# An order of instructions written out by hand and a scheduler, against a recorded one placed by a table of times

## The chip, the cores and the metric

The kernel runs on one core of a Trainium2 chip. The metric is device time in microseconds (us) of one execution; the median of three runs of the kernel before is 1881.01 us (1879.83 to 1881.45). Engines are named TensorE (PE in the profile), VectorE (DVE), ScalarE (ACT), GpSimd (POOL) and SyncE (SP, which only issues DMAs here). Each runs its own queue of instructions in order; semaphores make one wait for another.

## What is computed

A two-layer decoder trunk on x of 2048 positions by 1024 features, in float32. Layer 0 is a gated short convolution; then keys and values are projected once; layer 1 is stick-breaking attention of 8 heads of 64, with a gate.

```python
def _short_conv_mixer(h, w_in, w_conv, w_out):
    b_gate, c_gate, xin, g = jnp.split(h @ w_in, 4, axis=-1)
    y = b_gate * _causal_depthwise_conv(c_gate * xin, w_conv)
    return (y * jax.nn.silu(g)) @ w_out
...
    z = jnp.einsum("bhqd,bhkd->bhqk", qb, kf[:, :, :kl]) * scale
    log_one_minus = jnp.where(mask, jax.nn.log_sigmoid(-z), 0.0)
    rev = lax.cumsum(log_one_minus, axis=3, reverse=True)
    weights = jnp.exp(jnp.where(mask, z + rev, -jnp.inf))
    outs.append(jnp.einsum("bhqk,bhkd->bhqd", weights, vf[:, :, :kl]))
...
    x = x + (o * jax.nn.silu(g)) @ w_out_b[j]
return _rmsnorm(x, norm_f)
```

## The kernel before

Activations lie transposed (features on partitions, positions reversed along the free axis), so the causal sums run forward. Positions are cut into four chunks of 512 (CH). A matmul in full precision is made of three in fp32r: operands are split into a high and a low part (split, L163), and mm3 (L192) adds high x high, high x low, low x high: 24 matmuls of 128 x 512 for 1024 features. Weights are split once and stored to DRAM; later uses load 1 MB of both parts into one of four buffers (whl).

The stages, by function:
- mixer_in (L273) makes the gates C, X, B, G and the convolution: chunks 0 and 1 together (m01), then 2, then 3. Beside m01 run stats_x (square sums of chunks 2 and 3) and fold_gains (weights of later layers scaled and split).
- proj_out (L374) multiplies by w_out_a, adds x, normalizes; proj_k, proj_q, proj_v and proj_gate project, and their results go to DRAM.
- attention(c, h) (L477) takes a chunk of queries and a head, and walks the key chunks kc from c down to 0. For each of four blocks of 128 queries (qi): two matmuls make z (L498, L499); ScalarE makes R and w from it by two sigmoids (L501, L503); GpSimd copies the carry or masks the diagonal (L507 to L511); VectorE runs a multiplying scan over R (L512) and multiplies w by it (L516). Then, for each of four blocks of 128 keys (kb): TensorE transposes the four w into one PSUM bank wt (L524), ScalarE casts it to wth and VectorE makes the rest wtl (L165), and two matmuls add v times each to av (L533, L534).
- out_b and out_norm (L583, L605) are the output projection, the sum of squares, and the last normalization of chunks 0 to 2, where GpSimd multiplies (L612). out_b_last (L623) is chunk 3's: it holds three quarters of the projection, and the last quarter waits for the last head: its output times its gate (L566), 24 matmuls (pol), square sums, normalization, stores.

Rings of buffers limit how far anything runs ahead: z and wt have two PSUM banks each, "lin" two, av one; R 5, w 8, wth and wtl 2, whl 4, "ld" 5, "og" 8, "hl" 1.

What sets the order: every function is a generator that yields an estimate of its matmul time, and merge (L700) draws from several generators in proportion to fixed totals (L732 to L755), so that attention of one chunk stands among projections of the next. Manual dependencies ("pace", L201) hold the filling matmuls near the attention's in the last part. Under this program order a list scheduler with a timing model of its own then reorders the instructions of each engine.

Of the kernel before, what the change touches and what calls it, by code (L numbers as in the profile page):

```python
# [1 line left out]

# [22 lines left out]
F0, F1, F2, F3, F4 = 0.4, 0.5, 0.65, 0.4, 0.6  # L25
S2, S3, S4, S7 = 2.0, 0.5, 3.0, 2.0
YN = 2.0
YP = (10.0, 8.0, 6.0, 6.0)
DLY = 3.0
NB = 3  # L30
GRP, GRY, SLACK = 3, 6, 8
PACE = mybir.DependencyInfo(mybir.DependencyClass.NoSync, mybir.DependencyReason.DATA)

# [3 lines left out]
EPS = 1e-6  # L37

# [7 lines left out]
def kernel(  # L46
# [15 lines left out]
    nc = tc.nc  # L62

    const = ctx.enter_context(tc.tile_pool(name="const", bufs=1))
    psum = ctx.enter_context(tc.tile_pool(name="psum", bufs=2, space=bass.MemoryType.PSUM))
    dram = ctx.enter_context(tc.tile_pool(name="dram", bufs=1, space=bass.MemoryType.DRAM))
    sb = ctx.enter_context(tc.tile_pool(name="sb", bufs=2))

    ident = const.tile([P, P], F32, name="ident")
    make_identity(nc, ident)  # L70
# [116 lines left out]
    MM = 222.0  # L187

    anchors = []
    fine = [24, False]  # L190

    def mm3(ps, wts, a, kt=KD):  # L192

        hi, lo = wts[:, 0], wts[:, 1]
        n = 0
        for k in range(kt):
            for w, m in ((hi, 0), (hi, 1), (lo, 0)):
                ins = nc.tensor.matmul(ps, w[:, k, :], a[k][:, m, :], start=n == 0, stop=n == 3 * kt - 1)  # L198
# [4 lines left out]
                if n % fine[0] == 0 and n < 3 * kt:  # L203
                    yield MM * fine[0]

    def rest(n):
        return MM * (n - (n - 1) // fine[0] * fine[0])

# [40 lines left out]
    def stats_x(c):  # L249
# [6 lines left out]
        yield 1.0  # L256
# [16 lines left out]
    def mixer_in(cs):  # L273
        if len(cs) == 1:
            h[cs[0]] = norm_x(cs[0])
            yield YN * 24 * MM
        for cb in range(KD):
            wts = {}
            for c in cs:
# [5 lines left out]
                def gate(g, i):  # L285
# [16 lines left out]
                    yield from mm3(ps, wts[g], h[c])  # L302
                    return ps

                pc = yield from gate("C", 1)
                cps = t512(f"cs_{nm}")
                nc.scalar.copy(cps, pc)
                yield rest(24)
# [3 lines left out]
                px = yield from gate("X", 2)  # L312
# [3 lines left out]
                if c in late_acc:  # L316
                    if c not in late:
                        pB = yield from gate("B", 0)
                        late[c] = late_rms(c, late_acc[c])
# [3 lines left out]
                yield rest(24)  # L323
                if pB is None:
                    pB = yield from gate("B", 0)
# [7 lines left out]
                yield rest(24)  # L333
                pG = yield from gate("G", 3)
# [10 lines left out]
                yield rest(24)  # L345


    def fold_gains():

        for nm, src, gain in (("kv", w_kv, gains["kv"]), ("b", w_in_b[0], gains["b"])):  # L350
            for i in range(KD):
# [9 lines left out]
                yield 1.0  # L361
        for ob in range(KD):
# [7 lines left out]
            yield 0.5  # L370
# [3 lines left out]
    def proj_out(c):  # L374
# [9 lines left out]
        yield 0.0  # L384
        for ob in range(KD):
            wts = load_w(w_out_a[0][:, ob * P:(ob + 1) * P], ("o", ob), f"o{c}_{ob}")
            ps = lin(f"po_{c}_{ob}")
            yield from mm3(ps, wts, y)
# [6 lines left out]
            yield rest(24)  # L395
# [9 lines left out]
        yield YP[c] * 24 * MM  # L405

    def proj_k(c, kb):
        wts = load_w(None, ("kv", kb), f"k{c}_{kb}")
        ps = lin(f"pk_{c}_{kb}")
        yield from mm3(ps, wts, kept[c])  # L410
# [5 lines left out]
        yield rest(24)  # L416

    def proj_q(c, qb):
        wts = load_w(None, ("b", qb), f"q{c}_{qb}")
        ps = lin(f"pq_{c}_{qb}")  # L420
        yield from mm3(ps, wts, kept[c])
# [3 lines left out]
        yield rest(24)  # L425

    def proj_v(c, vb):
        wts = load_w(None, ("kv", 4 + vb), f"v{c}_{vb}")
        ps = lin(f"pv_{c}_{vb}")
        yield from mm3(ps, wts, kept[c])  # L430
# [7 lines left out]
        nc.sync.dma_start(out=v_d[c][:, :, 2 * vb:2 * vb + 2, :, :], in_=vt.bitcast(F32))  # L438
        yield rest(24) + 2 * MM

    def proj_g(c, gb):
        wts = load_w(None, ("b", 4 + gb), f"gg{c}_{gb}")
        ps = lin(f"pg_{c}_{gb}")
        yield from mm3(ps, wts, kept[c])
# [4 lines left out]
        yield rest(24)  # L449

    def proj_first(c):
        yield from proj_out(c)
        yield from proj_k(c, 0)
        yield from proj_q(c, 0)
        yield from proj_v(c, 0)

    def proj_rest(c):
        yield from proj_k(c, 1)
        yield from proj_q(c, 1)
        yield from proj_v(c, 1)  # L460
        yield from proj_v(c, 2)
        yield from proj_v(c, 3)
        for i in (2, 3):
            yield from proj_k(c, i)
            yield from proj_q(c, i)

    def proj_gate(c, again=True):
# [5 lines left out]
        for i in range(4):  # L473
            yield from proj_g(c, i)


    def attention(c, h, ot):  # L477
# [8 lines left out]
        for kc in range(c, -1, -1):  # L486
# [5 lines left out]
            nc.scalar.dma_start(out=vt.bitcast(F32), in_=v_d[kc][:, :, h, :, :])  # L492
            ws = []
            for qi in range(4):
# [23 lines left out]
                yield (1400.0 if diag else 1800.0) / 4  # L518
            for kb in range(3, -1, -1):
# [14 lines left out]
                ins = nc.tensor.matmul(av[:, 0:n], vs, wl[:, 0:n], start=False, stop=final)  # L534
                anchors.append(ins)
                if kb:
                    yield (1900.0 if diag else 3500.0) / 4
# [5 lines left out]
            yield (1900.0 if diag else 3500.0) / 4  # L543

    def attention_chunk(c, gated=True):
        for hb in range(NH // 2):
            ot = sb.tile([P, CH], F32, name=f"ot_{c}_{hb}", tag="ot", bufs=2)
            yield from attention(c, 2 * hb, ot)
            yield from attention(c, 2 * hb + 1, ot)
            nc.sync.dma_start(out=og_d[c][hb], in_=ot)  # L550
# [22 lines left out]
    def gated_in(c, ks=range(4)):  # L573
# [209 lines left out]
```

## Time and profile before

| | before |
|---|---|
| median of three runs | 1881.01 us |
| the profiled execution, its own time | 1879.53 us |
| its span, first to last instruction | 1877.6 us |
| mean granted TensorE clock | 0.978 |
| instructions | 24847 |
| moved by DMA | 464.63 MB, mean 247 GB/s |

In the table of engines, the busy time of TensorE includes the pipelined end of each matmul; what it can issue is read from start-to-start times. A row of groups has: line, engine, operation, output <- inputs, shape, count, then total busy us and mean ns of one, then the idle time before them and what ended most of it. A row of waits has: engine and line, what it waited for, total us, times, longest. In the timeline each row has start, duration, engine, line, operation, and in brackets the idle time before it and what ended that.

### The profile page before, as it was taken

The numbers are of one execution on the slowest core, as the hardware profiler recorded it, in microseconds if no ns is written. First come the engines' busy times: TensorE is split into PE (matmuls) and PEld (weight loads), VectorE is DVE, ScalarE is ACT, GpSimd is POOL, SyncE is SP. The second block draws the span as 40 slices with busy tenths as digits, with TensorE's granted clock in tenths as the row PEclk, the third lists the DMA queues.
The fourth block names the chain that finished last, engine by engine and source line by source line (L and its number), as shares of the span: only waits on it lengthen the run. The fifth ranks groups of instructions, "written<-read, shape, count | busy, mean of one in ns | idle before, by whom it ended". The sixth has DMA issues, their size and how long they took to land.

```text
span 1877.6 us, 24847 instructions
## 1 busy us (share of the span) xinstructions
PE 1778.2 (95%) x8312; PEld 1448.5 (77%) x8312; DVE 1242.5 (66%) x1830; ACT 773.3 (41%) x1493; POOL 432.9 (23%) x814
## 2 busy tenths in 40 slices
PE   7999999999999999999999999999998998987884
PEld 5888888888778878887888888888776886865573
DVE  7766643554243364478784477787868888799874
ACT  6423311231132142345443344454535555566542
POOL 5000000101021032032221122232223212357533
PEclk9999999999999999999999999999999999998887
DMA  9999995687978697867687765666586666878663
GB/s 295 326 297 326 330 308 168 213 311 277 337 253 285 219 324 264 286 220 250 208 253 237 257 201 187 196 200 214 186 291 202 212 205 233 275 235 261 224 203 131
DMA packets 240783, 464.63 MB, mean 247 GB/s; under 512 B 18704, under 2 KB 133392, under 8 KB 216080
## 3 DMA queue, kind: packets, MB, share of 16 engines
q1 hardware_dynamic: 180576, 404.28, 63.5%
q10 hardware_dynamic: 59920, 58.74, 11.0%
q8 instruction: 66, 1.08, 0.2%
q14 instruction: 61, 0.50, 0.1%
q0 software_dynamic: 160, 0.02, 0.1%
HBM read 326.92 MB, written 136.05 MB: 247 GB/s over the span
## 4 chain that ended last, share of the span: by engine, by line
PE 76%; DMA 9%; DVE 7%; issue 3%; ACT 2%; POOL 2%; SPq 0%; ACTq 0%; POOLq 0%; DVEq 0%
PE pG L198 9%; PE pB L198 9%; PE pX L198 9%; PE po L198 9%; PE pC L198 8%; PE pv L198 5%; PE wt L524 4%; PE pk L198 4%; PE pq L198 4%; PE pg L198 3%; PE av L534 3%; PE av L533 2%; DVE R L512 2%; PE z L498 2%; PE z L499 2%
## 5 line engine op out<-in xcount | busy, mean ns | idle before, releaser
L512 DVE TENSOR_TENSOR_SCAN R<-R,R,ones 128x512 f32<-128x512 f32 x192 | 252.5, 1317 | 32.2 <-ACT R L501 31.7
L501 ACT ACTIVATE R<-z 128x512 f32<-128x512 f32 (+1 forms) x320 | 174.2, 544 | 193.8 <-PE z L499 84.9
L165 DVE TENSOR_TENSOR wtl<-wt,wth 128x512 fp32r<-128x512 f32 (+1 forms) x320 | 186.5, 602 | 81.9 <-ACT wth L164 79.8
L164 ACT CAST wth<-wt 128x512 fp32r<-128x512 f32 (+1 forms) x320 | 160.8, 528 | 185.5 <-PE wt L524 167.4
L516 DVE TENSOR_TENSOR w<-w,R 128x512 f32<-128x512 f32 (+1 forms) x320 | 200.8, 637 | 24.9 <-POOL R L511 4.8
L198 PE MATMUL pC<-h,whl_C 128*128 128x512 f32 x768 | 191.4, 399 | 9.2 <-ACT whl_C L164 7.9
L511 POOL COPY R<-R 128x1 f32<-128x1 f32 x192 | 114.9, 599 | 346.5 <-DVE R L512 313.7
L198 PE MATMUL po<-y,whl_o 128*128 128x512 f32 x768 | 190.7, 394 | 2.7 <-DVE x L392 1.6
L198 PE MATMUL pX<-h,whl_X 128*128 128x512 f32 x768 | 188.1, 393 | 1.1 <-DVE cv L343 1.1
L198 PE MATMUL pG<-h,whl_G 128*128 128x512 f32 x768 | 185.7, 391 | 0.0
L198 PE MATMUL pB<-h,whl_B 128*128 128x512 f32 x768 | 185.6, 391 | 0.0
L524 PE MATMUL wt<-ident,w 128*128 128x128 f32 x1088 | 175.5, 276 | 7.2 <-DVE w L516 5.5
L198 PEld LDWEIGHTS pC<-h,whl_C 128*128 128x128 f32 x768 | 144.6, 191 | 43.6 <-ACT whl_C L164 7.9
L503 ACT ACTIVATE w<-z 128x512 f32<-128x512 f32 (+1 forms) x320 | 172.0, 542 | 2.8 <-PE wt L524 2.7
L198 PEld LDWEIGHTS pX<-h,whl_X 128*128 128x128 f32 x768 | 143.1, 188 | 32.3 <-DVE cv L343 1.3
L198 PEld LDWEIGHTS po<-y,whl_o 128*128 128x128 f32 x768 | 142.4, 188 | 33.2 <-DVE x L392 1.8
L198 PEld LDWEIGHTS pG<-h,whl_G 128*128 128x128 f32 x768 | 143.4, 188 | 30.2 <-issue 0.7
L198 PEld LDWEIGHTS pB<-h,whl_B 128*128 128x128 f32 x768 | 143.4, 188 | 29.8
L524 PEld LDWEIGHTS wt<-ident,w 128*128 128x128 f32 x1088 | 136.8, 142 | 35.7 <-DVE w L516 6.9
L512 DVE TENSOR_TENSOR_SCAN R<-R,ones 128x512 f32<-128x512 f32 (+3 forms) x128 | 117.2, 920 | 45.5 <-POOL R L507 39.2
L534 PE MATMUL av<-wtl,vv 128*128 128x512 f32 (+1 forms) x320 | 125.5, 395 | 19.9 <-DVE wtl L165 19.4
L498 PE MATMUL z<-kt,q 128*128 128x512 f32 (+1 forms) x320 | 128.1, 403 | 7.1 <-ACT w L503 7.0
(161 smaller groups left out, 2662.4 us busy)
## 6 DMA issues: line engine op xcount, KB each, us to landing
whl_o<-sw_o SPq DMA_DIRECT2D x24, 1024.0 KB, 5.3
kt<-k_d ACTq DMA_DIRECT2D x80, 256.0 KB, 3.7
vv<-v_d ACTq DMA_DIRECT2D x80, 256.0 KB, 4.5
whl_C<-sw_C SPq DMA_DIRECT2D x16, 1024.0 KB, 5.3
whl_X<-sw_X SPq DMA_DIRECT2D x16, 1024.0 KB, 5.0
whl_B<-sw_B SPq DMA_DIRECT2D x16, 1024.0 KB, 5.5
whl_G<-sw_G SPq DMA_DIRECT2D x16, 1024.0 KB, 5.4
whl_k<-sw_kv SPq DMA_DIRECT2D x16, 1024.0 KB, 6.7
```

Of the source, the lines that this page charges most:

```text
L164: nc.scalar.copy(hi, src)
L165: eng.tensor_sub(lo, src, hi.bitcast(F32))
L198: ins = nc.tensor.matmul(ps, w[:, k, :], a[k][:, m, :], start=n == 0, stop=n == 3 * kt - 1)
L498: nc.tensor.matmul(ps[:, lom:CH], q2[:, 0, qi * P:(qi + 1) * P], kt[:, lom:CH], start=True, stop=False)
L499: nc.tensor.matmul(ps[:, lom:CH], q2[:, 1, qi * P:(qi + 1) * P], kt[:, lom:CH], start=False, stop=True)
L501: nc.scalar.activation(R[:, lo + 1:CH + 1], ps[:, lo:CH], AF.Sigmoid, scale=-0.125)
L503: nc.scalar.activation(w[:, lo:CH], ps[:, lo:CH], AF.Sigmoid, scale=0.125)
L511: nc.gpsimd.tensor_copy(R[:, 0:1], carry[qi])
L512: nc.vector.tensor_tensor_scan(out=R[:, lo + 1:CH + 1], data0=R[:, lo + 1:CH + 1], data1=ones[:, 0:1].to_broadcast([P, CH - lo]), initial= ...
L516: nc.vector.tensor_mul(w[:, lo:CH], w[:, lo:CH], R[:, lo:CH])
L524: nc.tensor.transpose(wt[:, qi * P:(qi + 1) * P], ws[qi][:, kb * P:(kb + 1) * P], ident)
L534: ins = nc.tensor.matmul(av[:, 0:n], vs, wl[:, 0:n], start=False, stop=final)
```

## The change

The whole body is run once through stand-ins for pools, tiles and engines. They record each operation, with its part (78 names: m01, s2, a35 for chunk 3's head 5, o2 for chunk 2's output, and so on), its dependencies by overlapping regions, and an estimate of its cost. Generators, merge and the manual dependencies are gone. PLAN gives each part two times; a part's operations are spread evenly between them, which gives each a place. Then order() fills a table: again and again it takes, over all engines, the operation that can start earliest (ties by place), given its inputs, its engine, free buffers of its tag, turns between VectorE and GpSimd for operations on two SBUF tiles, and at most 8 DMAs in flight. The result is emitted in that order, under manual_schedule, which keeps it. All instructions therefore carry one line of the program.

```diff
+PLAN = {
+    "m01": (-696.3, -373.1), "s2": (116.9, 307.1), "s3": (-527.4, -474.4), "fold": (141.2, 142.2),
...
+        o.turns = not psum and sum(isinstance(v, View) for v in rest) > 1 and (kind == DVE or kind == POOL and n > 8)
...
+            o.key = t0 + (t1 - t0) * k / count[o.part]
...
+            for e, waiting in avail.items():
+                for o in waiting:
+                    t = max(o.ready, busy[e])
+                    if o.turns:
+                        t = max(t, turn[POOL if e == DVE else DVE])
+                    if o.late is None and len(landing) >= FLY:
+                        t = max(t, landing[-FLY])
+                    for b in o.bases:
+                        if b.tag:
+                            t = max(t, free[b.tag][turn_of[b]]) if turn_of[b] < len(free[b.tag]) else None
+                            if t is None:
+                                break
+                    if t is not None and (best is None or (t, o.place) < best[:2]):
+                        best = t, o.place, o
...
-    v_d = [dram.tile([P, 4, NH, 2, 64], F32, name=f"v_d_{c}") for c in range(NCH)]
+    v_d = [[dram.tile([P, 4, 2, 2, 64], F32, name=f"v_d_{c}_{h}") for h in range(NH // 2)] for c in range(NCH)]
...
+    x2_d = [[dram.tile([P, CH], F32, name=f"x2_d_{c}_{k}") for k in range(KD)] for c in range(NCH)]
...
-                ins = nc.tensor.matmul(ps, w[:, k, :], a[k][:, m, :], start=n == 0, stop=n == 3 * kt - 1)
-                if fine[1] and len(anchors) > SLACK and n % GRP == 0:
-
-                    tc.add_manual_dep(ins.ins, anchors[-1 - SLACK].ins.name, PACE, reason="pace")
+                nc.tensor.matmul(ps, w[:, k, :], a[k][:, m, :], start=n == 0, stop=n == 3 * kt - 1)
...
-            x = ld512(f"x1o_{c}_{ob}")
+            x = sb.tile([P, CH], F32, name=f"x1o_{c}_{ob}", tag="og", bufs=KD)
...
-        sg = load_sg(c, 3)
-        yield -1.0
+        sg = sb.tile([P, CH], F32, name=f"sgl_{c}", tag="hl", bufs=1)
+        nc.sync.dma_start(out=sg, in_=sg_d[c][3])
...
+    part("m01", mixer_in, (0, 1))
...
+    ops = nc.order(PLAN)
+    with tc.manual_schedule():
+        nc.emit(ops)
```

Three places show how rows move. The first is TensorE in chunk 3's head 2, where the key chunk 2 is transposed (wt_3_2_2_3: chunk 3, head 2, key chunk 2, key block 3) and multiplied (av), among the gate projections pg. Before:

```order
L533 MATMUL av_3_2_13846<-wth_3_2_2_3_14033,vv_3_2_2_13974 128x512
L198 MATMUL pg_0_0_14264<-xa_0_0_14246,whl_gg0_0_14262 128x512
L198 MATMUL pg_0_0_14264<-xa_0_1_14247,whl_gg0_0_14262 128x512 x3
L198 MATMUL pg_0_0_14264<-xa_0_2_14248,whl_gg0_0_14262 128x512 x3
L534 MATMUL av_3_2_13846<-wtl_3_2_2_3_14034,vv_3_2_2_13974 128x512
L524 MATMUL wt_3_2_2_1_14069<-ident_66,w_3_2_2_0_13981 128x128
L524 MATMUL wt_3_2_2_1_14069<-ident_66,w_3_2_2_1_13997 128x128
L524 MATMUL wt_3_2_2_1_14069<-ident_66,w_3_2_2_2_14007 128x128
L524 MATMUL wt_3_2_2_1_14069<-ident_66,w_3_2_2_3_14023 128x128
L498 MATMUL z_3_2_0_1_14271<-kt_3_2_0_14232,q2_3_2_13843 128x512
L533 MATMUL av_3_2_13846<-wth_3_2_2_2_14054,vv_3_2_2_13974 128x512
```

The same blocks now:

```order
L350 MATMUL wt_3_2_2_3_14082<-ident_66,w_3_2_2_3_14030 128x128
L350 MATMUL wt_3_2_2_2_14085<-ident_66,w_3_2_2_3_14030 128x128
L350 MATMUL z_3_2_1_2_14113<-kt_3_2_1_13897,q2_3_2_13346 128x512
L350 MATMUL pg_0_0_14110<-xa_0_0_12355,whl_gg0_0_13703 128x512 x2
L350 MATMUL pg_0_0_14110<-xa_0_1_12360,whl_gg0_0_13703 128x512
L350 MATMUL av_3_2_14033<-wth_3_2_2_3_14122,vv_3_2_2_14002 128x512
L350 MATMUL pg_0_0_14110<-xa_0_1_12360,whl_gg0_0_13703 128x512 x2
L350 MATMUL pg_0_0_14110<-xa_0_2_12369,whl_gg0_0_13703 128x512
L350 MATMUL z_3_2_1_3_14142<-kt_3_2_1_13897,q2_3_2_13346 128x512 x2
L350 MATMUL av_3_2_14033<-wtl_3_2_2_3_14135,vv_3_2_2_14002 128x512
L350 MATMUL av_3_2_14033<-wth_3_2_2_2_14126,vv_3_2_2_14002 128x512
L350 MATMUL av_3_2_14033<-wtl_3_2_2_2_14144,vv_3_2_2_14002 128x512
```

Before, the four transposes of one block stood together, and the products of a block came after the next block's transposes. Now both banks are filled at once, w by w, and the products follow after four to eight other matmuls.

The second place is the end of GpSimd's queue: products of chunk 2's output with its norm (x2r_2 by pbs_2), square sums of chunk 3 (acc_x23) and its last products (x2_3 by pbs_3). Before:

```order
L612 TENSOR_TENSOR x2r_2_6_17251<-x2r_2_6_17251,pbs_2_17225 128x512
L612 TENSOR_TENSOR x2r_2_7_17255<-x2r_2_7_17255,pbs_2_17225 128x512
L653 TENSOR_TENSOR acc_x23_0_17435<-acc_x23_0_17435,sq_x232_17454 128x512
L653 TENSOR_TENSOR acc_x23_0_17435<-acc_x23_0_17435,sq_x234_17470 128x512
L664 TENSOR_TENSOR x2_3_1_17118<-x2_3_1_17118,pbs_3_17522 128x512
L664 TENSOR_TENSOR x2_3_4_17121<-x2_3_4_17121,pbs_3_17522 128x512
L664 TENSOR_TENSOR x2_3_7_17124<-x2_3_7_17124,pbs_3_17522 128x512
```

Now:

```order
L350 TENSOR_TENSOR acc_x23_0_17446<-acc_x23_0_17446,sq_x234_17494 128x512
L350 TENSOR_TENSOR x2r_2_0_17412<-x2r_2_0_17412,pbs_2_17522 128x512
L350 TENSOR_TENSOR x2r_2_1_17418<-x2r_2_1_17418,pbs_2_17522 128x512
L350 TENSOR_TENSOR x2r_2_2_17451<-x2r_2_2_17451,pbs_2_17522 128x512
L350 TENSOR_TENSOR x2r_2_3_17482<-x2r_2_3_17482,pbs_2_17522 128x512
L350 TENSOR_TENSOR x2r_2_4_17498<-x2r_2_4_17498,pbs_2_17522 128x512
L350 TENSOR_TENSOR x2r_2_5_17545<-x2r_2_5_17545,pbs_2_17522 128x512
L350 TENSOR_TENSOR x2r_2_6_17550<-x2r_2_6_17550,pbs_2_17522 128x512
L350 TENSOR_TENSOR x2_3_1_16597<-x2_3_1_16597,pbs_3_17566 128x512
L350 TENSOR_TENSOR x2r_2_7_17559<-x2r_2_7_17559,pbs_2_17522 128x512
L350 TENSOR_TENSOR x2_3_4_17005<-x2_3_4_17005,pbs_3_17566 128x512
L350 TENSOR_TENSOR x2_3_7_17404<-x2_3_7_17404,pbs_3_17566 128x512
```

Chunk 2's eight products stood ahead of chunk 3's square sums; now they stand behind them, among the last products.

The third place is the SP queue, where the gate of the last two heads is loaded (sga_3_3 before, sgl_3 now). Before, near the end of its 864 rows, among the stores of chunk 2's output:

```order
L613 DMA out_0_dram<-x2r_2_4_17243 128x512
L611 DMA x2r_2_7_17255<-y_d_2_7_108 128x512
L613 DMA out_0_dram<-x2r_2_5_17247 128x512
L556 DMA sga_3_3_17429<-sg_d_3_3_232 128x512
L613 DMA out_0_dram<-x2r_2_6_17251 128x512
```

Now, 120 rows earlier, ahead of chunk 1's output projection:

```order
L350 DMA x2_d_0_4_249<-x1o_0_4_12656 128x512
L350 DMA sga_3_0_16001<-sg_d_3_0_241 128x512
L350 DMA sgl_3_16054<-sg_d_3_3_244 128x512
L350 DMA ogr_3_0_16061<-og_d_3_0_289 128x512
L350 DMA x1o_0_6_16074<-x1_d_0_6_123 128x512
```

The load no longer stands behind stores that wait for GpSimd.

In the order of heads, chunk 3's head 6 now comes last, after head 7, and chunk 2's output projection stands among chunk 1's and 3's.

More of the change, by code (lines that the diff above doesn't have):

```diff
@@ L1 @@
 from contextlib import ExitStack
+import numpy as np
 import concourse.bass as bass
@@ L37, with __init__, place @@
 EPS = 1e-6
+PLAN = {
[18 rows of a table added]
+}
+PE, ACT, DVE, POOL, SP = "tensor", "scalar", "vector", "gpsimd", "sync"
+SEM = 0.09
+DMA_RATE, DMA_BEFORE, DMA_AFTER, FLY = 0.36, 1.0, 1.4, 8
+class Base:
+    def __init__(self, pool, shape, dtype, kw):
+        self.pool, self.shape, self.dtype, self.kw = pool, list(shape), dtype, kw
+        self.tile = None
+        self.tag = (pool.kind, kw["tag"], kw["bufs"]) if kw.get("bufs") and pool.kind != "dram" else None
+        self.users = []
+    def place(self):
+        if self.tile is None:
+            self.tile = self.pool.real.tile(self.shape, self.dtype, **self.kw)
+        return self.tile
@@ L429, in proj_v @@
         ps = lin(f"pv_{c}_{vb}")
-        yield from mm3(ps, wts, kept[c])
+        mm3(ps, wts, kept[c])
         t = t512(f"vT_{c}_{vb}")
@@ L443, in proj_g @@
         ps = lin(f"pg_{c}_{gb}")
-        yield from mm3(ps, wts, kept[c])
+        mm3(ps, wts, kept[c])
         t = t512(f"sgb_{c}_{gb}")
@@ L448, in proj_g, with proj @@
         nc.sync.dma_start(out=sg_d[c][gb], in_=t)
[L449 to L465, printed above, removed]
+    def proj(c, i):
+        proj_k(c, i)
+        proj_q(c, i)
+        proj_v(c, i)
     def proj_gate(c, again=True):
@@ L533, in attention @@
                 nc.tensor.matmul(av[:, 0:n], vs, wh[:, 0:n], start=first, stop=False)
[L534 to L537, printed above, removed]
+                nc.tensor.matmul(av[:, 0:n], vs, wl[:, 0:n], start=False, stop=final)
             if kc == 0:
```

431 lines of the change are left out of this document (281 added, 150 removed), and 17 rows, old and new, of the table PLAN.

## The prediction

> **What bounds the kernel now.** First the page: the span, the busy shares and the granted clock in 40 slices.
>
> ```profile
> span 1877.6 us, 24847 instructions
> PE 1778.2 (95%) x8312; PEld 1448.5 (77%) x8312; DVE 1242.5 (66%) x1830; ACT 773.3 (41%) x1493; POOL 432.9 (23%) x814
> PEclk9999999999999999999999999999999999998887
> ```
>
> TensorE is busy for 95% of the span; 99.4 us of it is idle, and the clock sags at the end. So the question is where those 99.4 us lie. I cut the span at four matmuls at which each order has done the same TensorE work, with every matmul priced by its start-to-start time. The chain of waits prices a 512-wide matmul, the timeline a transpose:
>
> ```profile
> 57.91 5.44 PE pG L198 x24
> ...
> 1127.59 1.04 PE L524 MATMUL wt<-ident,w 128*128 128x128 f32 x8
> 1128.39 0.48 PE L498 MATMUL z<-kt,q 128*128 128x512 f32 x1
> 1128.70 0.40 PE L499 MATMUL z<-kt,q 128*128 128x512 f32 x1
> ```
>
> 5.44/24 is 0.227 us for 512 columns; eight transposes and one z take 1128.70 - 1127.59 = 1.11, so a transpose takes about 0.11; 384 and 256 columns in proportion. By these prices both orders hold the same 1712.6 us of TensorE work. Marks at 1300, 1350, 1600 and 1700 us of work fall in the trace at 1340.9, 1402.5, 1685.9 and 1833.4 us. The windows between them (columns: PE, PEld, DVE, ACT, POOL busy, clock, DMA):
>
> ```profile
> 0.00:1340.90 1340.90, 1319.18 (x6158) 1088.22 (x6159) 815.69 (x1220) 491.19 (x940) 231.76 (x518) 1.00 0.78 258
> 1340.90:1402.50 61.60, 55.28 (x266) 42.76 (x265) 46.96 (x79) 29.08 (x58) 17.07 (x26) 0.97 0.68 247
> 1402.50:1685.90 283.40, 261.43 (x1298) 211.37 (x1297) 236.23 (x320) 162.48 (x324) 87.68 (x164) 0.99 0.70 228
> 1685.90:1833.40 147.50, 123.47 (x536) 93.78 (x535) 124.24 (x175) 81.06 (x156) 82.84 (x97) 0.86 0.73 231
> 1833.40:1877.60 44.20, 18.80 (x60) 12.33 (x58) 19.39 (x38) 9.49 (x16) 13.54 (x11) 0.69 0.37 125
> ```
>
> Call them A to E. A does 1300 us of work in 1340.9: nearly matmul-bound. B does 50 in 61.6, C 250 in 283.4, D 100 in 147.5 and E 12.6 in 44.2. So 11.6, 33.4 and 47.5 us can be won in B, C and D, all in the stretch where chunk 3's attention runs. VectorE is at 83% of C and 84% of D. The waits of TensorE name it too:
>
> ```profile
> PE av L534 <- DVE wtl L165: 19.4, 19, 2.4
> PE pol L198 <- ACT og L164: 8.9, 1, 8.9
> PE pC L198 <- ACT whl_C L164: 7.9, 1, 7.9
> PE z L498 <- ACT w L503: 7.0, 9, 1.5
> PE pv L198 <- DVE khl L165: 6.7, 2, 5.3
> ```
>
> **The change, part by part.** No instruction comes or goes: both orders hold the same matmuls and the same VectorE rows. What changes is the order on every queue, three buffers, and v_d cut by head pairs. So each term is one of VectorE's load against TensorE's pace, stage by stage.
>
> VectorE's work per stage follows from the groups (count times mean ns), with the order's rows counted between the marks:
>
> ```profile
> L512 DVE TENSOR_TENSOR_SCAN R<-R,R,ones 128x512 f32<-128x512 f32 x192 | 252.5, 1317 | 32.2 <-ACT R L501 31.7
> L165 DVE TENSOR_TENSOR wtl<-wt,wth 128x512 fp32r<-128x512 f32 (+1 forms) x320 | 186.5, 602 | 81.9 <-ACT wth L164 79.8
> L516 DVE TENSOR_TENSOR w<-w,R 128x512 f32<-128x512 f32 (+1 forms) x320 | 200.8, 637 | 24.9 <-POOL R L511 4.8
> L512 DVE TENSOR_TENSOR_SCAN R<-R,ones 128x512 f32<-128x512 f32 (+3 forms) x128 | 117.2, 920 | 45.5 <-POOL R L507 39.2
> ```
>
> In C before: 68 full scans x 1.317 + 22 diagonal x 0.920 + 90 w x 0.637 + 85 wtl x 0.602 + 45 others at about 0.69 + 12 small ones at 0.16 = 251 us; the window shows 236 busy, 0.94 of it, since ends overlap. After: 72, 27, 98, 100 and 44 give 273, so 256 busy. In D before: 28, 8, 36, 42, 30 and 24 small give 117; the window shows 124, 1.06 of it. After: 24, 5, 30, 32, 31 and 24 give 100, so 106 busy. The order moves some 20 us of VectorE work from B and D into C, and D then has only 106 us of it against 100 of matmuls.
>
> **C**: 256 busy us are the floor if VectorE never waits; TensorE's own pace for C is 254 (A's 1319.18 busy us for 1300 of work, 1.015, times 250). Its fullest 50 us before show how near to that it can come:
>
> ```profile
> 1700.00:1750.00 50.00, 40.49 (x176) 30.85 (x174) 47.05 (x66) 29.27 (x58) 29.92 (x40) 0.83 0.79 246
> ```
>
> 47.05 of 50 is 0.94, which gives 256/0.94 = 272. At the 0.83 that C has now it would be 308. I take 266, between the floor and the full row and nearer to the row, since two transposed blocks now fill together and hand VectorE their work in pairs.
>
> **D**: 106 is its floor, 106/0.94 = 113, and 106/0.84 = 126 at today's share. GpSimd's multiplications of the output are in D and E as before, and they shut out VectorE's operations on two SBUF tiles:
>
> ```profile
> 1787.53 1.29 POOL L161 TENSOR_TENSOR acc_x<-acc_x,sq_x 128x512 f32<-128x512 f32 x1
> 1788.47 0.90 DVE L516 TENSOR_TENSOR w<-w,R 128x512 f32<-128x512 f32 x1
> ```
>
> The w product ends at 1789.37, 0.55 after the addition does, though it was issued 0.35 before that end: it waited. The new order puts wtl operations, which read PSUM, in pairs beside such GpSimd pieces. I take 119, midway between 113 and 126.
>
> **B**: its 46.96 busy VectorE us stand in 61.6; its work falls from 52 to 43. I take 51.5, a little over TensorE's pace (50 x 1.015). **A**: the two khl waits (6.7) and the like should shrink; the 7.9 at the start stays, as the first ten rows of the SP queue are the same. Against that, one stretch of 100 us of matmuls in chunk 2's heads now holds 109 us of VectorE's work by the prices above, where the fullest such stretch of A held 95. I take 1336, with 1327 to 1355 as bounds: all idle time but the start gone (1340.9 - 21.7 + 7.9), or 13.8 more of it.
>
> **E**: the load of the last gate moves from row 852 of the SP queue to row 732, into a buffer that nothing else holds by then.
>
> ```profile
> 1830.57 6.28 POOL L612 TENSOR_TENSOR x2r<-x2r,pbs 128x512 f32<-128x512 f32 x5 [17.01 <-ACT pbs L608]
> ...
> 1839.53 0.69 DVE L542 TENSOR_TENSOR ot<-ot,av 64x512 f32<-64x512 f32 x1 [0.61 <-ACT ot L541]
> ...
> 1842.12 0.33 SPq L556 DMA_DIRECT2D sga<-sg_d  x1
> ...
> 1846.39 0.69 DVE L566 TENSOR_TENSOR ot<-ot,sga 128x512 f32<-128x512 f32 x1 [6.17 <-DMA sga<-sg_d]
> ...
> 1860.72 1.86 PE L125 MATMUL pst_x<-ones,acc_x 128*128 128x1 f32 x8 [3.29 <-DVE acc_x L655]
> ...
> 1863.22 0.16 DVE L137 TENSOR_TENSOR t_x<-yr_x 128x4 f32<-128x4 f32 x1
> ...
> 1865.83 2.05 PE L147 MATMUL prb_x<-dg_x,ones 128*128 128x512 f32 x2 [3.25 <-DVE dg_x L146]
> ```
>
> The product with the gate then follows the addition at once: 6.2 us go. But chunk 2's normalization moves behind the last head. Its 12 small VectorE operations (0.16 and a gap, 0.2 each) stand among the eight final additions: about 2.4, partly in gaps. Its GpSimd products (6.28/5 = 1.26 each) stand seven in front of the first of the last chunk's three, and one between them. They can start about when the last statistic does (1860.72) and take 8.8; the last chunk's factor leaves TensorE at 1867.88 and needs a copy of 0.6, 7.8 after that start. So 1 to 2 us come on top. E becomes 44.2 - 6.2 + 2 = 40.
>
> The sum is 1336 + 51.5 + 266 + 119 + 40 = 1812.5 of span. The profiled execution took 1879.53, 1.9 more than its span, so 1814.4; its time lies 1.5 below the median of the three runs, which I leave.
>
> **The clock.** Half-speed stretches follow clusters of short waits:
>
> ```profile
> 518.20 0.50 PE L533 MATMUL av<-wth,vv 128*128 128x512 f32 x1 [0.47 <-ACT wth L164]
> 520.33 8.44 PE L198 MATMUL pv<-xn,whl_v 128*128 128x512 f32 x24 [1.63 <-DVE qhl L165]
> ```
>
> 24 matmuls took 8.44 instead of 5.44 after gaps of 0.47 and 1.63. The Trainium skill, in "TensorE: Matmul & The Clock Gate", section "HAM oscillation — how this bites in real kernels", says that only idle gaps over about 3.4 us close the gate. By that rule the short waits of the new order would cost no clock, D would stay at VectorE's 113 and the sum would fall to 1808; the trace shows it lower after shorter ones, so 119 stays.
>
> **The rivals.**
>
> *TensorE-bound throughout.* If the order hides everything, A keeps its 7.9 (1327), B, C and D run at 1.015 us per us of work (51, 254, 101.5), E 40: 1773.5, so 1775. For it: VectorE's floors (256, 106) are hardly above. Against: no 50 us of the trace shows VectorE over 0.94.
>
> *The load is level, but VectorE keeps its share.* At 0.83 and 0.84 C is 308 and D 126: 1336 + 51.5 + 308 + 126 + 40 = 1861.5, so 1863, still 0.9% faster. The even load saves nothing in C then, since C's work grows by 20 us.
>
> *No slack between transposes and products (slower).* By the orders and the matmul prices, the median distance from a block's last transpose to its wtl product was 6.0 us of other matmuls between 700 and 1340 us of work, and 4.8 in the last part. Now it is 2.2 and 2.4, and a tenth of the blocks have under 1.9. What it must cover:
>
> ```profile
> 1825.42 0.60 PE L524 MATMUL wt<-ident,w 128*128 128x128 f32 x4
> ...
> 1826.05 0.59 ACT L164 CAST wth<-wt 128x512 fp32r<-128x512 f32 x1 [2.16 <-PE wt L524]
> 1826.67 0.69 DVE L165 TENSOR_TENSOR wtl<-wt,wth 128x512 fp32r<-128x512 f32 x1 [0.60 <-ACT wth L164]
> ```
>
> The last transpose starts near 1825.75 and ends its turn 0.11 later; wtl is there at 1827.36: 1.5 us. The margin is 0.7 us at the median, less than one scan (1.32) that stands in front. Blocks come in 160 pairs; the order gains 65 us, so it is lost from 65/160 = 0.41 us per pair on. With a 0.6 us operation ahead each time it costs 96: 1910. Against: the waits for wtl now are 19.4 us in all, 0.12 per pair, and a waiting TensorE lets VectorE catch up. This is also how the change would fail to do what it says: the plan's times would not be the chip's.
>
> **How the numbers follow.** Forecast 0.66; TensorE-bound 0.11; share kept 0.13; slower 0.10. The forecast's own bounds are A 1327 to 1355, C 256 to 308 and D 106 to 147, seldom all at one end: 1790 to 1845. The range 1780 to 1866 takes in most of the second and third case. A measurement of this kernel tells about 0.2% from no change. Faster by more: 0.66 + 0.11 and most of 0.13, so 0.87; within it 0.04; slower 0.09.
>
> **What would show it.** Right: at the same marks C near 266 with VectorE over 0.92 of it, D near 119 with a clock above 0.9, the wait for sga gone, E near 40. The slower rival: waits of av for wtl in a hundred places and a clock under 0.95 in C. Wrong altogether: a wait for a weight load or for kt, which TensorE hardly has now, or A longer than before.

## The result, and the profile after

The changed kernel takes 1808.87 us (median; 1807.08 to 1809.78), beside 1880.42 for the kernel before on the same chip: a ratio of 0.9623, 95% interval 0.9605 to 0.9641. Its profiled execution took 1809.78 with a span of 1808.1. First its page, the lines that answer to those of before:

```profile
span 1808.1 us, 24782 instructions
PE 1755.3 (97%) x8312; PEld 1425.4 (79%) x8312; DVE 1234.5 (68%) x1830; ACT 777.2 (43%) x1493; POOL 418.5 (23%) x814
PEclk9999999999999999999999999999999999999996
```

Each engine has as many instructions as before; only the total is 65 lower. TensorE's idle time fell from 99.4 to 52.8 us and its busy time by 23 us, and the sag of the clock at the end is gone but for the last slice. The span cut at the same four marks of TensorE's work (columns as in the prediction):

```profile
0.00:1340.10 1340.10, 1322.06 (x6167) 1081.73 (x6168) 808.68 (x1225) 495.12 (x939) 230.91 (x515) 1.00 0.77 258
1340.10:1393.00 52.90, 51.42 (x251) 40.98 (x251) 45.67 (x69) 27.06 (x56) 13.11 (x31) 1.00 0.85 310
1393.00:1652.40 259.40, 257.67 (x1329) 209.32 (x1327) 252.81 (x341) 175.91 (x356) 93.55 (x181) 1.00 0.72 237
1652.40:1762.80 110.40, 105.47 (x511) 81.89 (x510) 101.21 (x147) 69.38 (x130) 60.64 (x73) 1.00 0.86 287
1762.80:1808.10 45.30, 18.71 (x60) 11.53 (x58) 26.13 (x51) 9.73 (x16) 20.31 (x16) 0.67 0.64 206
```

| stage | before | predicted | after |
|---|---|---|---|
| A | 1340.9 | 1336 | 1340.1 |
| B | 61.6 | 51.5 | 52.9 |
| C | 283.4 | 266 | 259.4 |
| D | 147.5 | 119 | 110.4 |
| E | 44.2 | 40 | 45.3 |

The gain lies in B, C and D: 9, 24 and 37 us. Of D's 37, 18 are TensorE's busy time (123.47 us before, 105.47 after, for the same work), as the clock granted there rose from 0.86 to 1.00; the other 19 are idle time that went. VectorE is busy for 252.81/259.4 = 97% of C (83% before) and 92% of D (84%). The waits of TensorE (total, times, longest):

```profile
PE prb_x L350 <- DVE dg_x L350: 9.9, 2, 6.6
PE pC L350 <- ACT whl_C L350: 8.0, 1, 8.0
PE wt L350 <- DVE w L350: 3.4, 5, 1.3
PE av L350 <- DVE wtl L350: 2.0, 5, 0.6
```

Products wait 2.0 us for wtl instead of 19.4. On top now is prb_x, the last norm of the program: E.

### The profile page after: what moved, and what is told of

Same layout as the page of the kernel before. It is cut to its first block, busy times and chain, and to the rows that moved or that the text cites. A ratio compares the mean times of both kernels' runs of the same rounds, so it can differ in the third digit from the quotient of the medians.

```text
span 1808.1 us, 24782 instructions
## 1 busy us (share of the span) xinstructions
PE 1755.3 (97%) x8312; PEld 1425.4 (79%) x8312; DVE 1234.5 (68%) x1830; ACT 777.2 (43%) x1493; POOL 418.5 (23%) x814
## 4 chain that ended last, share of the span: by engine, by line
PE 79%; DVE 9%; DMA 6%; issue 4%; ACT 1%; POOL 1%; SPq 0%; ACTq 0%; POOLq 0%; DVEq 0%
PE pB L350 9%; PE pG L350 9%; PE pC L350 9%; PE po L350 8%; PE pX L350 8%; PE av L350 6%; PE z L350 6%; PE wt L350 5%; PE pk L350 5%; PE pv L350 4%; PE pq L350 4%; PE pg L350 3%; PE pob L350 3%; DVE R L350 3%; DVE w L350 2%
## 5 line engine op out<-in xcount | busy, mean ns | idle before, releaser
L350 ACT ACTIVATE R<-z 128x512 f32<-128x512 f32 (+2 forms) x320 | 173.6, 544 | 150.3 <-PE z L350 114.0
L350 ACT CAST wth<-wt 128x512 fp32r<-128x512 f32 (+2 forms) x320 | 156.1, 526 | 178.7 <-PE wt L350 146.2
L350 DVE TENSOR_TENSOR wtl<-wt,wth 128x512 fp32r<-128x512 f32 (+2 forms) x320 | 181.8, 598 | 64.9 <-ACT wth L350 61.4
L350 PE MATMUL z<-kt,q 128*128 128x512 f32 (+2 forms) x640 | 207.8, 387 | 1.8 <-DMA kt<-k_d 1.0
L350 PE MATMUL pB<-h,whl_B 128*128 128x512 f32 x768 | 208.3, 395 | 1.1 <-ACT whl_B L350 1.0
L350 PE MATMUL pG<-h,whl_G 128*128 128x512 f32 x768 | 207.1, 395 | 0.0
L350 DVE TENSOR_TENSOR w<-w,R 128x512 f32<-128x512 f32 (+2 forms) x320 | 201.3, 642 | 5.4 <-POOL R L350 0.5
L350 ACT ACTIVATE w<-z 128x512 f32<-128x512 f32 (+2 forms) x320 | 171.8, 544 | 49.9 <-PE z L350 48.0
L350 PEld LDWEIGHTS wt<-ident,w 128*128 128x128 f32 x1088 | 139.6, 140 | 44.4 <-DVE w L350 10.9
L350 DVE TENSOR_TENSOR_SCAN R<-R,ones 128x128 f32<-128x128 f32 (+3 forms) x128 | 112.2, 885 | 40.8 <-POOL R L350 39.4
L350 PEld LDWEIGHTS z<-kt,q 128*128 128x128 f32 x640 | 112.3, 189 | 20.4 <-ACT w L350 1.8
```

The source lines that it names most:

```text
L350: getattr(o.engine.engine, o.name)(*map(real, o.args), **{k: real(v) for k, v in o.kw.items()})
```

## The experiments

Times in us; the ratio is to the kernel before on the same chip, and stages are cut at the same marks of work. The stages are those of the one profiled execution, whose own time lies up to 8 us from the median (e11's took 1884.1).

| run | time | ratio (95%) | A | B | C | D | E |
|---|---|---|---|---|---|---|---|
| after | 1808.9 | 0.9605 to 0.9641 | 1340.1 | 52.9 | 259.4 | 110.4 | 45.3 |
| e1 old places | 1863.4 | 0.9895 to 0.9928 | 1360.6 | 57.6 | 264.7 | 140.6 | 41.3 |
| e2 norm early | 1821.3 | 0.967 to 0.970 | 1339.0 | 53.0 | 259.1 | 122.3 | 47.0 |
| e3 less slack | 1938.2 | 1.0283 to 1.0322 | 1414.9 | 61.2 | 293.1 | 121.3 | 49.3 |
| e4 no turns | 1836.9 | 0.9742 to 0.9784 | 1345.8 | 52.1 | 272.5 | 122.2 | 43.2 |
| e5 half of e3 | 1846.8 | 0.9782 to 0.9845 | 1361.6 | 53.4 | 265.7 | 117.0 | 44.4 |
| e6 more slack | 1834.1 | 0.972 to 0.9786 | 1343.2 | 53.0 | 261.9 | 128.3 | 45.5 |
| e7 no flight | 1843.0 | 0.976 to 0.9827 | 1363.9 | 57.2 | 262.9 | 118.1 | 45.4 |
| e8 norm cut | 1804.6 | 0.9551 to 0.9614 | 1338.1 | 53.1 | 260.0 | 112.8 | 38.9 |
| e9 jitter a | 1834.5 | 0.9723 to 0.9763 | 1348.6 | 57.6 | 266.1 | 109.5 | 46.1 |
| e10 jitter b | 1828.8 | 0.9685 to 0.9725 | 1347.9 | 53.4 | 262.9 | 116.6 | 46.0 |
| e11 gate load | 1876.5 | 0.996 to 0.9995 | 1342.4 | 65.4 | 287.8 | 147.9 | 38.5 |
| e12 norm in PSUM | 1808.5 | 0.9591 to 0.962 | 1337.9 | 53.0 | 259.7 | 113.1 | 44.8 |

### The places of the plan

e1 gives each part of PLAN the stretch of TensorE work that it had in the order before:

```diff
-    "a36": (1788.6, 1802.2), "a37": (1752.7, 1777.4),
+    "a36": (1610.6, 1644.0), "a37": (1644.2, 1705.4),
```

> PLAN alone is replaced: each part gets the stretch of TensorE work that it filled in the order before; recorder, table of engines, buffers and loads stay. By the prices of the groups VectorE then has 62 us of work in B, 243 in C, 122 in D (now 43, 273, 100). Theory of the load (the gain of C and D comes from spreading VectorE's work by the plan): D at VectorE's 0.92 is 122/0.92 = 132 instead of 110, B 62, C at TensorE's pace 257, A and E as they are: about 1835. Rival, the fine order (two transposed blocks filled together, products from the table, whatever stands where): stages as now, 1808 to 1816. Rival, the plan is all (an uneven plan returns to the time before): 1865 to 1880.

Measured: 1863, 28 above the theory of the load and just under the range of its second rival. C and D of e1:

```profile
1418.20:1682.90 264.70, 259.17 (x1301) 208.79 (x1300) 235.13 (x312) 164.12 (x328) 89.73 (x163) 1.00 0.71 239
1682.90:1823.50 140.60, 121.27 (x530) 89.05 (x529) 130.87 (x183) 80.53 (x152) 78.08 (x95) 0.90 0.74 238
```

D shows the load: VectorE has 130.87 us of work there instead of 101, at 93% of the stage, and D is 30 us longer. That is the larger part of the 55 us that the places are worth. A lost 20 more, which the load does not explain (VectorE's work in A is 806.54, the same). And the rest of the change, with the places of before, still beats the kernel before by 16 us: C is 19 shorter than before, although VectorE has as much work there (235.13 us, and 236.23 before). So C's gain is not the load's. What went in C is waits of TensorE: 21 us in all before, 5 in e1, 2 with the change. The two longest of before, and then the longest of e1:

```profile
PE av L534 <- DVE wtl L165: 8.8, 8, 2.4
PE pv L198 <- DVE khl L165: 5.3, 1, 5.3
```
```profile
PE av L350 <- DVE wtl L350: 1.5, 3, 0.7
```

Which part of the fine order removes them was not tried.

### The slack between transposes and products

The planner believes a time from ScalarE's or VectorE's start to the moment another engine can use the result. e3 makes it 0.4 us shorter:

```diff
-            o.late = o.busy + 0.1 + SEM
+            o.late = o.busy - 0.3 + SEM
...
-            o.late = o.busy + 0.085 + SEM
+            o.late = o.busy - 0.315 + SEM
```

> The planner's latencies of ScalarE and VectorE are 0.4 us shorter, so products stand closer behind the transposes: median distance 1.7 us instead of 2.3, a tenth under 1.0, where copy and remainder need 1.5. Theory of the slack (the prediction's slower rival): about half the 160 pairs wait 0.3 us or more, waits of av for wtl rise from 2 to 30 us or more, time 1830 to 1850. Rival, TensorE's waits let VectorE catch up and the load decides: VectorE's work by stage is 51, 274, 96, so C and D stay within 3 us, waits for wtl under 10 us, 1808 to 1815.

Measured: 1938, worse than the kernel before, and far more than the theory of the slack had expected. The span is 132 us longer, and only 41 of these are idle time of TensorE; the other 91 are shown as busy (1846.3 us instead of 1755.3). So most of the loss is not in the table of waits, which names 5.8 us for av on wth and 2.1 on wtl. Stages A and C of e3, and the same matmuls by form in e3 and then after (busy us, mean ns | idle before):

```profile
0.00:1414.90 1414.90, 1371.64 (x6166) 1064.15 (x6167) 809.34 (x1226) 500.04 (x939) 216.56 (x515) 1.00 0.73 244
1476.10:1769.20 293.10, 284.51 (x1326) 204.77 (x1325) 253.36 (x342) 176.70 (x348) 77.82 (x180) 0.99 0.62 204
```
```profile
L350 PE MATMUL av<-wth,vv 128*128 128x512 f32 x224 | 99.5, 444 | 8.2 <-ACT wth L350 4.1 <-DVE ot L350 0.6 <-DMA vv<-v_d 0.5
```
```profile
L350 PE MATMUL av<-wth,vv 128*128 128x512 f32 x224 | 89.2, 398 | 0.0
```

TensorE "works" 50 us longer in A for the same matmuls. A matmul's shown duration (0.40) is longer than its turn (0.227), so a delay under some 0.17 us leaves no idle gap; it makes PE look busier. Measured from start to start, less the price of the matmul before, the delays between 0.05 and 1 us sum to 209 us in e3 and 78 in the changed kernel: the difference is the whole loss of 130. (The edit shortens the latency of every operation of the two engines, so not all of these delays are at the products.)

e5 takes half the step (0.2 us).

> The planner's latencies of ScalarE and VectorE are 0.2 us shorter (half of the last cut, which cost 130 us): median distance from transposes to product 2.0 us, a tenth under 1.5, VectorE's work by stage 46, 273, 96. In the last cut TensorE's start-to-start delays between 0.05 and 1 us summed to 209 us against 78, nearly all of the loss, and 237 of 640 products of av started late against 46. Theory of the slack, with a knee where copy and remainder (1.5 us) plus what stands ahead of them no longer fit: a third of that loss or less, 1825 to 1855, late products 80 to 150. Rival, in proportion to the latency: half the loss, 1865 to 1885. Rival, only the shortest distances count (under 1.0): 1808 to 1815.

Measured: 1847, inside the range of the knee. Delays of 0.05 to 1 us sum to 112, 33 more than after, and the span is 34 longer. Products of av that start over 0.05 us late: 46 after, 100 in e5, 237 in e3. e6 goes the other way, 0.5 us longer:

> The same latencies 0.5 us longer: median distance 3.2 us instead of 2.3, a tenth under 2.2. VectorE's work by stage becomes 45, 251, 116, since heads end later. Theory that slack is enough now and VectorE's load decides: late products fall a little, C runs at TensorE's pace 255 to 259, D at VectorE's 0.92 is 126, time 1820 to 1828. Rival, more slack still pays: the 78 us of delays between 0.05 and 1 us shrink by 10 or more and the time falls to 1795 to 1803.

Measured: 1834, above the 1820 to 1828 expected, with D at 128.3 where 126 was expected. Late products did not fall but rose, from 46 to 71, and the delays from 78 to 89 us. More slack does not pay: heads end later and VectorE's work moves back to D. Here C and D of e6:

```profile
1396.20:1658.10 261.90, 257.63 (x1304) 209.98 (x1302) 238.64 (x319) 164.54 (x331) 102.09 (x168) 1.00 0.76 249
1658.10:1786.40 128.30, 113.29 (x534) 85.46 (x532) 120.46 (x171) 76.66 (x148) 70.32 (x90) 0.96 0.75 244
```

120.46 of 128.3 is 94%: VectorE is the bound of D here. It is not the only one that D has: in e2, e3 and e4 D takes 121 to 122 us with 99 to 104 us of VectorE's work.

### Turns, flights, and a control

e4 and e7 each take one piece of knowledge from the table; e9 and e10 take none, and only disturb PLAN.

```diff
-                    if o.turns:
-                        t = max(t, turn[POOL if e == DVE else DVE])
```

> The table no longer makes VectorE and GpSimd take turns for operations on two SBUF tiles; everything else stays. If this knowledge carries the gain, collisions (0.55 us in the one that the trace before showed) on some 140 GpSimd operations of C to E stretch VectorE's work, C and D grow by 20 to 40 us: 1828 to 1848. Rival, it matters little, because VectorE's own order is decided by the data: its work by stage is 52, 278, 91, which by 0.97 and TensorE's pace gives B 55, C 265, D 102, and the sum stays at 1805 to 1812.

```diff
-DMA_RATE, DMA_BEFORE, DMA_AFTER, FLY = 0.36, 1.0, 1.4, 8
+DMA_RATE, DMA_BEFORE, DMA_AFTER, FLY = 0.36, 1.0, 1.4, 10000
```

> The limit of 8 DMAs in flight is taken from the table; engines' turns and latencies stay. VectorE's work by stage is 45, 275, 96, the distance from transposes to products as now. If the limit carries part of the gain, loads issued early stand in front of those needed and TensorE waits for weights, kt or vv by 10 us or more: 1820 to 1840. Rival, the queues hold only what the table's buffers let through, so the limit hardly bites: waits for DMA stay under 5 us, 1804 to 1812.

```diff
-    "a36": (1788.6, 1802.2), "a37": (1752.7, 1777.4),
+    "a36": (1788.7, 1802.3), "a37": (1752.3, 1777.0),
```

> A control: each part's two times in PLAN are moved together by a random amount between -2 and +2 us; the table, its latencies, turns and flights stay. VectorE's work by stage becomes 52, 275, 94 (now 43, 273, 100), the distance from transposes to product stays (median 2.3, a tenth under 1.6). If the losses of the runs without turns, without the flight limit and with other latencies (25 to 37 us) come from what they took away, this costs 10 us at most: 1806 to 1820. Rival, the plan fits only these exact numbers and any disturbance costs as much: 1830 to 1850.

> The same control with another draw: VectorE's work by stage 45, 268, 102, distances as now. If what was taken away decides: 1806 to 1820. Rival, any disturbance costs as much: 1830 to 1850.

The controls cost 26 and 20 us, in A (8 each), B and C or D, at no one place. e9 lies in the rival's range and e10 just under it, both over the 1820 that was the limit of the other reading: the rival holds. Their delays of 0.05 to 1 us sum to 91 and 89, 11 to 13 over the change, and 41 to 43 products of av are late: what e3 showed (209 us, 237) is slack and not disturbance. e5 (112 us, 100) shows slack too, but of its 38 us only the 12 to 18 that the controls do not cost are shown to be its price. PLAN's numbers fit one exact order, and a loss of 20 to 26 us says nothing of what an edit took away. So e4's 28, e6's 25 and e7's 34 are not shown to be the price of turns, of slack that is too long, or of flights, though e4's time lies in the range of its theory. Their own marks have to be read instead. e6's mark is D, 18 longer with 19 more of VectorE's work. For e4 there are VectorE's products of two SBUF tiles in C and D, in e4 and then after:

```profile
L348 DVE TENSOR_TENSOR w<-w,R 128x512 f32<-128x512 f32 (+3 forms) x128 | 95.1, 753 | 2.1
L348 DVE TENSOR_TENSOR og<-ogr,og 128x512 fp32r<-128x512 f32 x15 | 12.2, 823 | 0.1
```
```profile
L350 DVE TENSOR_TENSOR w<-w,R 128x512 f32<-128x512 f32 (+3 forms) x128 | 91.5, 725 | 1.6 <-POOL R L350 0.5
L350 DVE TENSOR_TENSOR og<-ogr,og 128x512 fp32r<-128x512 f32 x15 | 10.3, 685 | 0.0
```

Without turns they take 5.5 us longer in all, and in the controls, which keep the turns, no longer than after (101 and 100 us). But with the scans, which read SBUF tiles alone as well, VectorE takes 257.5 us after, 264.9 in e4, and 259.2 and 263.5 in the controls. So some 5 us may be the collisions' own; that is not shown, and the rest is open. e7 is open altogether: waits for DMA stayed small, as the rival said, but its time did not, and its profile was odd even where no head runs yet. The first row is e7's, the second after's, 100 us each with the clock granted in full:

```profile
100.00:200.00 100.00, 100.00 (x430) 80.46 (x429) 69.93 (x99) 34.04 (x51) 4.40 (x9) 1.00 1.01 344
```
```profile
100.00:200.00 100.00, 100.00 (x443) 82.82 (x442) 70.88 (x101) 34.24 (x50) 5.00 (x9) 1.00 1.02 354
```

430 matmuls against 443. It stays so: 433 against 445 between 300 and 400 us, where e7 moves fewer bytes than the changed kernel (196 GB/s against 223), and over the whole trace even the fastest tenth of the 512-wide matmuls follow each other after 0.230 us instead of 0.226. By that ratio some 30 of the 39 us that this execution lost (1.8% of 1713 us of work, an estimate) are a slower TensorE at the same granted clock, and not the order. The cause is open.

### The tail

e11 takes the load of the last gate alone, in the kernel before:

```diff
-        sg = load_sg(c, 3)
+        sg = sb.tile([P, CH], F32, name=f"sgl_{c}", tag="hl", bufs=1)
+        nc.sync.dma_start(out=sg, in_=sg_d[c][3])
```

> The kernel before with one part of the change alone: the last gate is loaded into the buffer of the ring hl, so its load stands at row 666 of SP's queue instead of 852. The prediction's term: the product with the gate no longer waits 6.2 us, E falls from 44.2 to 38 and the time by 0.33% to 1873 to 1875. Rival: the tail then waits for something else (the additions or GpSimd), E falls by 3 us or less, under 0.16%.

Measured: E 38.5, and 0.05 to 0.4% faster. In time alone that leaves room for the rival; E decides, where the product with the gate no longer waits:

```profile
1850.34 0.69 DVE L566 TENSOR_TENSOR ot<-ot,sgl 128x512 f32<-128x512 f32 x1
```

The term holds. So E's 45.3 with the change is 7 us of new cost. In the changed kernel, VectorE and GpSimd at the end:

```profile
1785.48 6.15 POOL L350 TENSOR_TENSOR x2r<-x2r,pbs 128x512 f32<-128x512 f32 x5 [5.38 <-ACT pbs L350]
...
1787.36 0.16 DVE L350 TENSOR_SCALAR v_x<-pst_x 128x4 f32<-128x4 f32 x1 [2.58 <-PE pst_x L350]
...
1788.03 1.19 DVE L350 TENSOR_SCALAR yr_x<-t_x 128x4 int32<-128x4 int32 x1
1789.25 1.18 DVE L350 TENSOR_TENSOR t_x<-yr_x 128x4 f32<-128x4 f32 x1
...
1793.06 0.69 DVE L350 TENSOR_TENSOR dg_x<-yr_x,ident 128x512 f32<-128x512 f32 x1
...
1793.37 1.51 POOL L350 TENSOR_TENSOR x2r<-x2r,pbs 128x512 f32<-128x512 f32 x1 [1.74 <-DMA x2r<-x_d]
...
1797.95 1.26 POOL L350 TENSOR_TENSOR x2r<-x2r,pbs 128x512 f32<-128x512 f32 x1
1799.17 2.48 POOL L350 TENSOR_TENSOR x<-x,pbs 128x512 f32<-128x512 f32 x2
```

Two things are seen: operations of 0.16 us take 1.2 while GpSimd multiplies, and chunk 2's eight products last from 1785.48 to 1799.2. e2 moves them ahead, by PLAN:

```diff
-    "o2": (1737.2, 1875.3), "o3": (1759.4, 1903.3), ...
+    "o2": (1760.0, 1835.0), "o3": (1800.0, 1903.3), ...
...
-    ... "n2": (1901.4, 2143.9), ...
+    ... "n2": (1895.0, 1899.0), ...
```

> Three entries of PLAN move chunk 2's output and its normalization ahead, so that its twelve small VectorE operations stand before the last eight additions and most of its GpSimd products end before the last statistic. If these are what E lost against the prediction (the small operations of the last norm took 1.2 us instead of 0.16 beside GpSimd's products), E falls from 45.3 to 39 to 41 and the time to 1803 to 1805. Rival: E is bound by the chain of the last head (gate, 24 matmuls, additions, squares, norm, products) and the stretched operations lie beside it; E stays at 44 to 46, time 1807 to 1811.

A miss on both sides: D grew by 12, and E did not fall (47.0). SyncE's queue and TensorE in e2, and then SyncE after:

```profile
1745.06 10.33 SPq L350 DMA_DIRECT2D x2r<-x_d  x4
...
1788.07 0.53 SPq L350 DMA_DIRECT2D whl_obl<-sw_ob  x1
```
```profile
1772.61 2.30 PE L350 MATMUL pob<-og,whl_ob 128*128 128x512 f32 x9 [1.13 <-DMA whl_ob<-sw_ob]
1781.38 0.77 PE L350 MATMUL pol<-og,whl_obl 128*128 128x512 f32 x1 [3.05 <-DMA whl_obl<-sw_ob]
1789.74 5.94 PE L350 MATMUL pol<-og,whl_obl 128*128 128x512 f32 x15 [3.39 <-DMA whl_obl<-sw_ob]
```
```profile
1769.90 0.53 SPq L350 DMA_DIRECT2D whl_obl<-sw_ob  x1
```

The norm's loads (x2r) wait at the head of SyncE's queue, 10.33 us for four, and the last weights are issued behind these and later ones: the last at 1788 instead of 1770. TensorE's waits for these weights, 6.4 us, lie in E and cost what the norm may have won there. They do not explain D, which ends at 1773.4: TensorE idles 12.3 us in it instead of 4.9, no single wait over 3.4, and the cause stays open (e2 disturbs PLAN as well). e8 leaves the products out, so that chunk 2's output is not the kernel's, and e12 cures the stretching alone:

```diff
-            nc.gpsimd.tensor_mul(t, t, pbs)
+            if c != 2:
+                nc.gpsimd.tensor_mul(t, t, pbs)
```

> GpSimd's eight products of chunk 2's last normalization are left out (that chunk's output is stored without its norm). If they stretched the last norm (1.2 instead of 0.16 us for an operation) and the chain from the last statistic to the end, E falls from 45.3 to 39 to 42 and the time to 1803 to 1806. Rival: the tail waits for the chain of the last head anyway, the stretched operations excepted: E 43 to 45, 1806 to 1809.

```diff
-            y = sb.tile([P, 4], F32, name=f"yr_{nm}", tag="sy")
+            y = ps[:, 4:8] if nm == "x23" else sb.tile([P, 4], F32, name=f"yr_{nm}", tag="sy")
...
+                nc.vector.scalar_tensor_tensor(out=t, in0=y, scalar=-0.5, in1=v, op0=ALU.mult, op1=ALU.mult)
+                nc.vector.tensor_mul(t, y, t)
```

> Last norm of chunk 3 alone: its iterate lies in PSUM and each small VectorE operation reads at most one SBUF tile (same count, the products regrouped); rows up to the last statistic are those of the change. If operations on SBUF alone are held by GpSimd's products, all twelve take 0.16 to 0.25 us, the last norm ends 4 us earlier and E falls to 41 to 43 (GpSimd's eleven products, 1.25 each, then end the program), 1804.5 to 1807. Rival: VectorE's small operations wait for GpSimd wherever their operands lie; E stays at 45, 1808 to 1810.

e8: E 38.9, as expected; there the last norm is not stretched either, and GpSimd's last three products end at 1797.4:

```profile
1793.69 3.72 POOL L350 TENSOR_TENSOR x<-x,pbs 128x512 f32<-128x512 f32 x3 [13.22 <-ACT pbs L350]
```

e12, VectorE's first and last operations of the norm and GpSimd's last product:

```profile
1788.05 0.16 DVE L350 TENSOR_SCALAR v_x<-pst_x 128x4 f32<-128x4 f32 x1 [2.58 <-PE pst_x L350]
...
1789.12 0.17 DVE L350 SCALAR_TENSOR_TENSOR pst_x<-t_x,pst_x 128x4 f32<-128x4 f32 x1
...
1790.50 0.69 DVE L350 TENSOR_TENSOR dg_x<-pst_x,ident 128x512 f32<-128x512 f32 x1
```
```profile
1800.84 1.26 POOL L350 TENSOR_TENSOR x2r<-x2r,pbs 128x512 f32<-128x512 f32 x1 [0.59 <-DMA x2r<-x_d]
```

The stretching is cured: 0.16 to 0.17 each, and from v_x to dg_x the norm takes 2.45 us instead of 5.70. The time is the same all the same: E 44.8, since GpSimd's last product ends at 1802.1 (1801.7 with the change). So curing the small operations alone is worth nothing: GpSimd's queue at the end, fed through five buffers, ends as late without them. What the queue costs alone, with the norm still stretched, was not tried, as e8 takes both away. e12 with the last chunk's three GpSimd products given to VectorE, which is idle from 1797.4, would follow from this; it was not tried. No run that computes everything is faster than the change by more than the interval.

## Why the prediction came out, step by step

The forecast 1814.4 stands 5.5 above 1808.9, and the order of the stages' gains is as forecast. That the sum is so near is in part luck: A, B and E came out 11 us above their terms, C and D 15 below.

- **C and D** took 7 and 9 us less than their terms. The load of VectorE was a little too high (256 and 106 busy us forecast, 252.81 and 101.21 measured), and the share that it reaches, taken between the full row's 0.94 and the floor in C and midway between 0.94 and 0.84 in D, too low: 0.97 and 0.92. By these, the load makes 3 of C's 7 us and 5 of D's 9, the share the rest.
- In **C** the share is not what sets the time. TensorE is busy for 257.67 of 259.4 us, near the 254 of its own pace, and e1 and e6, with 14 to 18 us less of VectorE's work there, are no shorter (264.7 and 261.9). The rival "TensorE-bound" was nearer in this stage (254 against 266). The prediction took VectorE's load against TensorE's pace as the whole of C; the waits that the order took away are its gain.
- In **D**, e8 and e12, whose rows are the same up to the last eight additions, take 113 us, so 2 to 3 of the 9 can change from run to run. Both had one half-speed stretch there (clock 0.98) that the changed kernel's profiled execution lacks; here e12's:

```profile
1759.39:1762.80 3.41, 3.41 (x12) 2.64 (x11) 0.89 (x2) 1.25 (x2) 3.41 (x3) 0.50 0.65 181
```

- **D** again: e1 and e6 show that the load is a cause there, as the prediction had it: with 131 and 120 us of VectorE's work, D is 140.6 and 128.3, at 93 and 94%.
- **The slower rival** did not come true, but it was near. It put the margin at 0.7 us at the median and the point of no gain at 0.41 us per pair. Taking 0.2 us of the margin cost 38 us (0.24 per pair, disturbance included), taking 0.4 cost 129 (0.81 per pair), slower than before. Its signs were wrong, though: in e3 av waits for wtl 10 times and 2.1 us in all, and the clock in C is 0.99. Most of the loss (91 of 132 us) came as late starts that leave no gap.
- **A**: 1340.1 instead of 1336 (1338 in e8 and e12). The start's wait stayed at 8.0, as said; short waits of 1.8 to 2.1 us came in place of those that went. TensorE's idle time fell by 3.7 us, its busy time rose by 2.9.
- **B**: 52.9 instead of 51.5.
- **E** is the term that came out the other way (a loss of 1 us where a gain of 4 was forecast): 6.2 less for the gate (5.7 in e11), but chunk 2's norm behind the last head was put at 2 and cost 7.3, since two things were taken as quick. GpSimd's seven products in front of the last chunk's first were put at 8.8 us in a row and took 11.3, with gaps of 1.74 and 0.62, because the last three loads wait for buffers. And the last chunk's factor was put at 7.8 us after the last statistic starts and was ready 11.1 after it, as the small operations were stretched. Without the products E is 6.4 shorter (e8), without the stretching alone 0.5 (e12).
- **The clock** fell to half speed twice in A, each time after one short wait (1.79 and 2.08 us); the first:

```profile
933.88 0.50 PE L350 MATMUL pk<-xn,whl_k 128*128 128x512 f32 x1 [1.79 <-DVE p L350]
```
```profile
931.00:935.10 4.10, 2.31 (x11) 1.58 (x10) 4.10 (x6) 1.32 (x2) 2.00 (x3) 1.00 0.94 302
935.10:938.50 3.40, 3.40 (x12) 2.83 (x12) 2.92 (x6) 0.54 (x2) 0.39 (x2) 0.50 0.75 227
```

A wait of 1.79 us, then 3.4 us at half speed. The Trainium skill's rule of gaps over about 3.4 us ("TensorE: Matmul & The Clock Gate", section "HAM oscillation — how this bites in real kernels") does not cover these. The sum that the prediction gave by that rule, 1808, is near the time all the same, but for another reason: D's waits went, and with them its half-speed stretches (clock 0.86 before, 1.00 after), and VectorE's load came out 5 us lower than forecast.

## What to carry to other kernels

An order planned ahead lives by the latencies that the planner believes: 0.4 us too little cost more than the whole gain, and 91 of these 132 us hide in TensorE's busy time, where only start-to-start times show them. Before an ablation of a planned order is believed, disturb the plan without taking anything away: here that alone cost 20 to 26 us, and four of the ablations 25 to 38. And price work that is moved behind the end by its queue with the buffers and loads that feed it, not by the sum of its durations.

## What the runs showed of the hardware

VectorE's small operations beside GpSimd's products took 1.18 to 1.19 us instead of 0.16, one with a single SBUF input (TENSOR_SCALAR on 128x4 int32) as well, which the planner does not count among its turns; with the iterate in PSUM none was held (0.16 to 0.17). This agrees with the Trainium skill, "SBUF — State Buffer", section "🔬 SBUF: two separate sides", by which the loser of the shared port waits for the winner's whole instruction: each held operation took about one product's turn (6.15/5 = 1.23). Why the TENSOR_SCALAR was held no run here shows.
